# The low part of every second ffn_down k-tile: an accumulating DMA onto the negated high part instead of a VectorE subtraction

## The chip, the cores and the metric

The kernel runs on one core of one Trainium2 chip. The metric is the device time of one execution, in microseconds (us). The kernel before takes 2200.96 us, the median of three runs (2200.92 to 2201.33). The engines are named as the profile names them: PE is TensorE (PEld its weight loads), ACT is ScalarE, DVE is VectorE, POOL is GpSimd, and SP is SyncE, whose queue issues the loads. "q" behind a name (SPq) is the engine's queue.

## The reference

Two layers of a bidirectional encoder over 256 tokens with 2048 channels, all in float32. Each layer adds two normed branches to the residual: a mixer of four parallel head groups between one input and one output projection, and a dense SwiGLU feed-forward of hidden width 5632. The change concerns the last product of the feed-forward alone:

```python
h = rmsnorm(x, norm_ffn_pre[l])
f = (jax.nn.silu(h @ ffn_gate[l]) * (h @ ffn_up[l])) @ ffn_down[l]
x = x + rmsnorm(f, norm_ffn_post[l])
```

`ffn_down[l]` is 5632 x 2048 in float32, 46 MB for each layer.

## The kernel before

All large products are made in float32r, a shortened float32, which the program's own estimate counts at a quarter of float32's time. To keep the precision, each operand is split into a high part (the value rounded to float32r) and a low part (what is left), and three products are summed: high by high, high by low, low by high. The weights stream through once from DRAM, and are split on the way:

- A *raw* tile holds two k-tiles of 128 rows by 1024 columns, 1 MB in all. SP issues its load (line 214). There are three raw tiles (`NRAW`).
- A *unit* is one k-tile with 1024 columns. `half` says which half of its raw tile it is: 0 or 1. Its high part, named `whi`, is a copy by ACT with conversion (line 227). Its low part, named `wlo`, is for ffn_down a subtraction by DVE, raw minus high (line 236). There are seven buffers of each (`NSPLIT`).
- A *step* is one unit's products with one of the two token tiles: six matmuls of 128x128 by 128x512 into two PSUM banks. In each bank the first matmul takes `whi`, the second takes `wlo`, and at the end the low part of the activations (`hT`) meets `whi` again.

In ffn_down the units run in groups of four. A group's four units are multiplied with token tile 0, then with token tile 1, so eight steps make a group. A unit's buffers come free after its step with token tile 1. Numbering the units of a group 4g to 4g+3, the buffers of unit 4g go to unit 4g+7, and so on. There are 176 units of ffn_down in the program: 2 layers, 2 halves of the output columns (`pair`), 44 k-tiles. So there are 44 groups, 22 in a row in each layer, and 88 units with `half` 1.

The order of the work on each engine is written out by the program itself. `run` walks the steps; before each, `splits_to` splits as many units ahead as there are free buffers. It emits the high part of unit n, then the low part of unit n-1. After the low part of a unit with `half` 1, `lo_next` emits the load that goes into the raw tile just finished, three raw tiles on:

```python
self.split_lo(self.units[self.next_lo])
self.next_lo += 1
if self.next_lo % 2 == 0:
    self.loads_to(self.next_lo // 2 + NRAW)
```

Each engine works through its own list in order, and waits are on data and buffers alone. So ACT's next high part waits until PE has finished with a buffer; DVE's low part waits for the high part; SP's load waits until the raw tile's last reader is done; and in the first matmuls of a step PE waits for the unit's high and low parts. The engine wrappers (`Paced`) also keep an estimate of each engine's progress, by which small side work (transposes, norms) is put between the products. Line 89 of the profile is the call in that wrapper, so nearly all compute instructions carry it, and rows are told apart by their tiles.

Of the kernel before, what the change touches and what calls it, by code (L numbers as in the profile page):

```python
# [11 lines left out]
F32 = mybir.dt.float32  # L12
F32R = mybir.dt.float32r
AF = mybir.ActivationFunctionType
ALU = mybir.AluOpType
# [19 lines left out]

SLOTS = 14  # 8 KB tiles for activations and what one mixer needs
NRAW = 3  # loads of two k-tiles of weights
NSPLIT = 7  # units of weights, split
RAMP = 3  # units split ahead at the start
CONV_LEAD = 1.5  # DVE's queue is filled up to here with the convolution's taps  # L40
LATENCY = 0.4  # from the end of side work to what depends on it
LC_AT = 12
STATS_AT = 20
IN_ORDER, OUT_ORDER = "BCADV", "CBAD"  # groups of w_in's columns, of w_out's rows
# Units by group: a group's products with one token tile follow those with the other.
START, FIRST, REGULAR, LAST = [2, 2, 4, 4, 4], [6, 5, 5], [4, 4, 4, 4], [4, 4, 3, 5]
# The first transposes of x: before which step, of which token tile and chunk
FIRST_X = ((0, 0, 0), (1, 1, 0), (6, 0, 1), (10, 1, 1), (13, 0, 2), (17, 1, 2), (21, 0, 3), (25, 1, 3))


class Unit:
    """One k-tile of weights for 1024 output columns."""

# [5 lines left out]
class Raw:  # L59
    """Two k-tiles of weights as they come from DRAM: parts are (columns' AP, width)."""  # L60

# [5 lines left out]
class Step:  # L67
    """One unit's products with one token tile, for some of its two banks."""

# [6 lines left out]
class Paced:  # L76
    """An engine that keeps an estimate of when its instructions so far will be done."""

# [24 lines left out]
class Trunk:  # L103
# [25 lines left out]

# [1 line left out]
    def name(self, s):  # L131
# [24 lines left out]

# [1 line left out]
    def spend(self, engine, op, n, args, kw):  # L158
# [26 lines left out]

# [1 line left out]
    def rsqrt(self, out, sums, n, inv):  # L187
        """out = (sums * inv + EPS) ** -0.5"""
        nc = self.nc
        m = self.small(n, "ms")  # L190
        nc.vector.tensor_scalar(m, sums, inv, EPS, op0=ALU.mult, op1=ALU.add)
        nc.gpsimd.tensor_tensor(out, m, self.mhalf[:, 0:n], op=ALU.pow)

    def split_hi_lo(self, dst, src):
        """dst[:, 0], dst[:, 1] = the float32r part of src, and what is left."""
        hi, lo = dst
        self.nc.scalar.activation(hi, src, AF.Copy)
        self.nc.vector.tensor_tensor(lo, src, hi.bitcast(F32), op=ALU.subtract)

# [1 line left out]
    def load(self, r, between):  # L201
        """Two k-tiles in one transfer for each part, or in two with other loads between them."""
        r.tile = self.wp.tile([P, 2, 1024], F32, tag="raw", bufs=NRAW, name=self.name("raw"))
        off = 0
        for ap, width in r.parts:
            src = ap[r.k * P:(r.k + 2) * P, :].rearrange("(k p) n -> p k n", p=P)
            dst = r.tile[:, :, off:off + width]
            if between:
                self.nc.sync.dma_start(dst[:, 0:1], src[:, 0:1])
                for f in between:  # L210
                    f()
                self.nc.sync.dma_start(dst[:, 1:2], src[:, 1:2])
            else:
                self.nc.sync.dma_start(dst, src)
            off += width
# [15 lines left out]
    def split_lo(self, u):  # L231
        self.chain = 0.0
        u.lo = self.wp.tile([P, 1024], F32R, tag="lo", name=self.name("wlo"))
        w, gain, hi = u.raw.tile[:, u.half, :], u.raw.gain, u.hi.bitcast(F32)
        if gain is None:
            self.nc.vector.tensor_tensor(u.lo, w, hi, op=ALU.subtract)
        else:
            self.nc.vector.scalar_tensor_tensor(
                u.lo, w, gain[:, u.k:u.k + 1], hi, op0=ALU.mult, op1=ALU.subtract
            )  # L240

    def splits_to(self, n, needed):
        """Splits weights up to unit n; the low part of one goes with the high part of the next."""
        n = min(n, len(self.units))
        while self.next_split < n:
            r = self.next_split // 2
            self.loads_to(r + 1)
            self.split_hi(self.units[self.next_split])
            if self.next_split > self.next_lo:
                self.lo_next()  # L250
            self.next_split += 1
        while self.next_lo < min(needed + 1, n):
            self.lo_next()
# [29 lines left out]
    def lhs(self, phase, k, tok):  # L283
        """The stationary operand, its two parts, and what must have been made before."""
        kind, l = phase
# [27 lines left out]

# [1 line left out]
    def spawn(self, g):  # L315
        self.gens.append([g, 0.0])

    def tick(self):
        """Carries each piece of side work on whose last instructions should be done by now."""
        todo, self.gens = self.gens, []  # L320
# [18 lines left out]
    def fill(self):  # L339
        """The convolution's taps, where DVE would have to wait otherwise."""  # L340
        if self.conv_work and self.at["DVE"] < self.at["PE"] + CONV_LEAD:
# [20 lines left out]

# [1 line left out]
    def constants(self):  # L364
# [12 lines left out]
    def tables(self):  # L377
        """Rotary tables and the window, from the host."""
        t = self.cp.tile([P, 832], F32, name="tables")
# [35 lines left out]

# [1 line left out]
    def square_sum(self, src, out, n=(512,), bias=0.0):  # L417
# [3 lines left out]
    def transpose_x(self, phase, tok, c):  # L421
        """Chunk c (4 k-tiles) of token tile tok of x, into xT."""
        nc = self.nc
# [39 lines left out]
    def first_x(self):  # L463
        """The first transposes, each some steps before its products, then the statistics."""
        def stats(tok):
# [8 lines left out]

# [1 line left out]
    def squares(self, phase, pair, tok, b):  # L476
# [10 lines left out]
    def post_banks(self, phase, pair, tok, banks):  # L487
        """Squares and gained values of a pair's banks."""
        for b in banks:
# [39 lines left out]

# [1 line left out]
    def ffn_half(self, phase, j, tok):  # L531
# [18 lines left out]

# [1 line left out]
    def layer_consts(self, l):  # L552
        """What one layer's mixer needs beside the weights, in one slot."""
        nc, a = self.nc, self.a
# [40 lines left out]
    def load_bias(self, l):  # L595
        """Relative position bias by query, head and key, keys of a row from the last to the first."""
        nc = self.nc
# [16 lines left out]

    # group B: convolution
    def glu(self, phase, pair, tok):
# [73 lines left out]
    def conv_norm(self, t, y, dst):  # L690
        """dst = silu(layer norm of y over the channels), one token tile, channels first."""
        nc, v = self.nc, self.v
# [27 lines left out]

    # rotated q and k of group A
    def rope_a(self, phase, pair, tok):
# [25 lines left out]
    def heads_transposed(self, dst, src, n):  # L748
        """dst[:, h, tok] = src(tok)[:, h] transposed, for n heads."""
        nc = self.nc  # L750
# [10 lines left out]
    def exps(self, p, src, nm, sm, scale):  # L761
        """p = exp(scale * src + nm), with its sums."""
        for t in range(T):
# [3 lines left out]
    def probs_transposed(self, p, dst):  # L767
        """dst[key, key tile, query] of p[query, query tile, key]."""
        nc = self.nc
# [51 lines left out]

    # group C
    def norm_c(self, phase, pair, tok):
# [46 lines left out]
    def softmax(self, p, src, scale):  # L870
        """p = softmax(scale * src) by row; two stages."""
        nc = self.nc
# [9 lines left out]
    def values(self, dst, h, v, pt):  # L882
        """dst[:, hi|lo, h] = the output of one head, transposed."""
        nc = self.nc
# [30 lines left out]

    # group D
    def evac_d(self, phase, pair, tok):
# [42 lines left out]

    # values of groups A and D, the last columns of w_in
    def evac_v(self, phase, pair, tok):
# [54 lines left out]

# [1 line left out]
    def with_rstd(self, phase, tok, g):  # L1019
# [14 lines left out]

# [1 line left out]
    def build(self):  # L1036
# [60 lines left out]
def shape_tables():  # L1097
    """Rotary tables and the columns' window: they depend on shapes alone."""
    f = np.float32
# [22 lines left out]
def by_partition(x, n):  # L1122
    """(..., n * 128) as (..., 128, n)"""
    return x.reshape(*x.shape[:-1], n, P).swapaxes(-1, -2)
# [28 lines left out]
```

## Time and profile before

| | us |
|---|---|
| median of three runs | 2200.96 |
| span of the profiled execution | 2199.3 |
| PE busy in it | 2177.8 |
| DVE busy | 1259.3 |
| ACT busy | 1095.4 |
| POOL busy | 28.6 |

The span runs from the first instruction of the profiled execution to its last; no other time of that execution is given. The median of the runs is 1.66 us above the span. Matmuls are pipelined, so one of them lasts longer than the distance to the next, and PE's busy time is where matmuls are under way. A wait is idle time of an engine, put down to what released it last. "To landing" is the time from a DMA's issue to its completion. The granted clock of PE, PEclk, is shown as a share of its full speed.

### The profile page before, as it was taken

Reading aid. Unit: us, or ns where it says so; the run is one execution under the profiler, and the core shown is the slowest. Engines: PE = TensorE matmul, PEld = TensorE weight load, DVE = VectorE, ACT = ScalarE, POOL = GpSimd, SP = SyncE. Lnnn points to the kernel's source line nnn. Section 1 sums busy time; section 2 is a strip of 40 time slices with the busy share of each in tenths; the row PEclk is TensorE's granted clock in tenths of the full one; section 3 lists DMA queues with packets and bytes.
Section 4 is the critical chain, followed back from the end, with each engine's and each line's share of the span. In section 5 each row is a group of like instructions: output and inputs, shape, how many; then the busy total and the mean of one; then the engine's idle time right before and its main releaser. Section 6 shows DMA issues by size and latency. Waiting matters only on the chain.

```text
span 2199.3 us, 25310 instructions
## 1 busy us (share of the span) xinstructions
PE 2177.8 (99%) x9896; PEld 1797.7 (82%) x9896; DVE 1259.3 (57%) x1498; ACT 1095.4 (50%) x1420; POOL 28.6 (1%) x38
## 2 busy tenths in 40 slices
PE   8999999999999999999999999999999999999998
PEld 6888887888888888888878888878888888888886
DVE  5898455545555554444478975565555555544444
ACT  5556655544444444343465576455444444443432
POOL 0000000000000000000000000000000000000000
PEclk9999999999999999999999999999999999999999
DMA  7556445655555555555565553655555555555553
GB/s 280 197 173 187 159 165 200 223 193 188 183 189 191 191 191 191 211 191 191 211 236 191 182 181 134 227 186 202 191 190 191 192 191 192 191 192 211 191 209 135
DMA packets 170007, 424.43 MB, mean 193 GB/s; under 512 B 18592, under 2 KB 19104, under 8 KB 167584
## 3 DMA queue, kind: packets, MB, share of 16 engines
q1 hardware_dynamic: 169744, 422.79, 55.7%
q8 instruction: 77, 1.26, 0.2%
q14 instruction: 42, 0.34, 0.0%
q10 hardware_dynamic: 144, 0.03, 0.0%
HBM read 414.40 MB, written 8.39 MB: 192 GB/s over the span
## 4 chain that ended last, share of the span: by engine, by line
PE 96%; ACT 1%; DVE 1%; DMA 1%; issue 0%; SPq 0%; DVEq 0%; POOLq 0%; ACTq 0%
PE acc L89 91%; PE tp L89 4%; PE sc L89 1%; DMA raw<-in_w_in_dram 1%; ACT whi L89 1%; DVE xT L89 0%; ACT workA L89 0%; DVE x L89 0%; ACT xT L89 0%; ACT L89 0%; DVE mx L89 0%; DVE wlo L89 0%; ACT conv L89 0%; ACT qkD L89 0%; ACT junk L89 0%
## 5 line engine op out<-in xcount | busy, mean ns | idle before, releaser
L89 PE MATMUL acc<-whi,xT 128*128 128x512 f32 x4096 | 1304.7, 394 | 7.7 <-ACT xT L89 3.1
L89 PEld LDWEIGHTS acc<-whi,xT 128*128 128x128 f32 x4096 | 769.3, 188 | 172.6 <-DVE xT L89 5.5
L89 DVE SCALAR_TENSOR_TENSOR wlo<-raw,gains,whi 128x1024 fp32r<-128x1024 f32 x512 | 651.7, 1281 | 344.3 <-ACT whi L89 331.0
L89 ACT ACTIVATE whi<-raw,gains 128x1024 fp32r<-128x1024 f32 x512 | 586.3, 1152 | 472.4 <-PE acc L89 448.8
L89 PE MATMUL acc<-wlo,xT 128*128 128x512 f32 x2048 | 799.4, 390 | 0.5 <-DVE wlo L89 0.5
L89 DVE TENSOR_TENSOR wlo<-raw,whi 128x1024 fp32r<-128x1024 f32 x240 | 293.5, 1224 | 274.0 <-ACT whi L89 256.2
L89 PEld LDWEIGHTS acc<-wlo,xT 128*128 128x128 f32 x2048 | 385.3, 188 | 77.2 <-DVE wlo L89 1.0
L89 PE MATMUL acc<-whi,hT 128*128 128x512 f32 x1408 | 434.5, 389 | 0.0
L89 ACT ACTIVATE whi<-raw 128x1024 fp32r<-128x1024 f32 x240 | 254.2, 1061 | 313.8 <-PE acc L89 313.7
L89 PEld LDWEIGHTS acc<-whi,hT 128*128 128x128 f32 x1408 | 264.3, 188 | 54.9
L89 PE MATMUL acc<-wlo,hT 128*128 128x512 f32 x704 | 273.9, 389 | 0.0
L89 PEld LDWEIGHTS acc<-wlo,hT 128*128 128x128 f32 x704 | 132.1, 188 | 27.4
L89 DVE SCALAR_TENSOR_TENSOR conv<-uT,lc,conv 128x256 f32<-128x256 f32 x240 | 99.2, 477 | 0.0
L89 DVE SCALAR_TENSOR_TENSOR h<-acc,rstd,h 128x512 f32<-128x512 f32 x44 | 33.0, 751 | 115.1 <-ACT h L89 114.5
L89 ACT ACTIVATE h<-acc,rstd 128x512 f32<-128x512 f32 x44 | 30.3, 689 | 81.7 <-PE acc L89 81.4
L89 DVE TENSOR_TENSOR hT<-tp,hT 128x512 fp32r<-128x512 f32 x44 | 30.4, 691 | 41.1 <-ACT hT L89 41.1
L89 ACT ACTIVATE junk<-acc 128x512 bf16<-128x512 f32 x32 | 19.0, 595 | 55.4 <-PE acc L89 53.3
L89 PE MATMUL acc<-whi,mixC 128*128 128x512 f32 x128 | 44.7, 402 | 0.0
L89 ACT ACTIVATE hT<-tp 128x512 fp32r<-128x512 f32 x44 | 25.8, 587 | 33.7 <-PE tp L89 33.7
L89 PE MATMUL acc<-whi,mixB 128*128 128x512 f32 x128 | 42.2, 397 | 0.0
L89 DVE TENSOR_TENSOR mg<-acc,gpost 128x512 f32<-128x512 f32 x32 | 21.4, 686 | 36.0 <-PE acc L89 19.3
L89 PE MATMUL acc<-whi,mixD 128*128 128x512 f32 x128 | 41.6, 391 | 0.0
(137 smaller groups left out, 978.1 us busy)
## 6 DMA issues: line engine op xcount, KB each, us to landing
raw<-in_ffn_gate_dram SPq DMA_DIRECT2D x176, 512.0 KB, 3.8
raw<-in_ffn_up_dram SPq DMA_DIRECT2D x176, 512.0 KB, 4.9
raw<-in_ffn_down_dram SPq DMA_DIRECT2D x88, 1024.0 KB, 5.0
raw<-in_w_in_dram SPq DMA_DIRECT2D x63, 1024.0 KB, 5.1
raw<-in_w_out_dram SPq DMA_DIRECT2D x32, 1024.0 KB, 5.0
raw<-in_w_in_dram SPq DMA_DIRECT2D x34, 512.0 KB, 4.6
x_spill<-x SPq DMA_DIRECT2D x6, 1024.0 KB, 8.2
x<-x_spill SPq DMA_DIRECT2D x6, 1024.0 KB, 9.1
```

Source lines behind the costliest of these rows:

```text
L89: return f(*args, **kw)
```

## The change

Outside this hunk the diff only removes comments. In ffn_down, units with `half` 1 no longer have their low part made by DVE. ACT writes the negated high part into the `wlo` buffer (a second copy with conversion of the raw tile, with scale -1), and then POOL issues a DMA that reads the raw tile in SBUF and adds it onto that buffer in SBUF: raw minus high.

```diff
         w, gain, hi = u.raw.tile[:, u.half, :], u.raw.gain, u.hi.bitcast(F32)
-        if gain is None:
+        if gain is None and u.phase[0] == "down" and u.half == 1:
+            self.nc.scalar.activation(u.lo, w, AF.Copy, scale=-1.0)
+            self.tc.nc.gpsimd.dma_start(u.lo.bitcast(F32), w, accum_op=ALU.add)
+        elif gain is None:
             self.nc.vector.tensor_tensor(u.lo, w, hi, op=ALU.subtract)
```

On ACT in the middle of layer 0's ffn_down, these rows stand before. `whi` is a high part, `raw` the raw tile it comes from, and two rows in a row share a raw tile (half 0, half 1):

```order
L89 ACTIVATE whi_6870<-raw_6792 128x1024
L89 ACTIVATE whi_6880<-raw_6816 128x1024
L89 ACTIVATE whi_6916<-raw_6816 128x1024
L89 ACTIVATE whi_6926<-raw_6862 128x1024
L89 ACTIVATE whi_6938<-raw_6862 128x1024
L89 ACTIVATE whi_6948<-raw_6884 128x1024
```

At the same place these stand now (the tiles have other numbers):

```order
L89 ACTIVATE whi_6884<-raw_6804 128x1024
L89 ACTIVATE whi_6894<-raw_6829 128x1024
L89 ACTIVATE wlo_6896<-raw_6804 128x1024
L89 ACTIVATE whi_6931<-raw_6829 128x1024
L89 ACTIVATE whi_6941<-raw_6876 128x1024
L89 ACTIVATE wlo_6943<-raw_6829 128x1024
L89 ACTIVATE whi_6954<-raw_6876 128x1024
L89 ACTIVATE whi_6964<-raw_6899 128x1024
L89 ACTIVATE wlo_6966<-raw_6876 128x1024
```

The negated copy of a raw tile's second unit (`wlo_6896` from `raw_6804`) stands behind the high part of the next unit, which comes from the next raw tile (`whi_6894` from `raw_6829`).

On SP, the loads of ffn_down with what they wait for, before (DVE's semaphore, and DMAHW, the completions of earlier SP transfers):

```order
L214 DMA raw_6884<-in_ffn_down_dram 128x2x1024 [waits DMAHW0_49,DVE_49]
L214 DMA raw_6930<-in_ffn_down_dram 128x2x1024 [waits DMAHW2_49,DVE_49]
L214 DMA raw_6952<-in_ffn_down_dram 128x2x1024 [waits DMAHW3_49,DVE_49]
L214 DMA raw_6998<-in_ffn_down_dram 128x2x1024 [waits DMAHW4_49,DVE_49]
L214 DMA raw_7020<-in_ffn_down_dram 128x2x1024 [waits DMAHW5_49,DVE_49]
```

The same loads now (DMASW is the completion of a DMA that POOL issued):

```order
L214 DMA raw_6899<-in_ffn_down_dram 128x2x1024 [waits DMASW6_49,DMAHW0_49,DVE_49,Activation_49]
L214 DMA raw_6946<-in_ffn_down_dram 128x2x1024 [waits DMASW7_49,DMAHW2_49,DVE_49,Activation_49]
L214 DMA raw_6969<-in_ffn_down_dram 128x2x1024 [waits DMASW0_49,DMAHW3_49,DVE_49,Activation_49]
L214 DMA raw_7016<-in_ffn_down_dram 128x2x1024 [waits DMASW1_49,DMAHW4_49,DVE_49,Activation_49]
L214 DMA raw_7039<-in_ffn_down_dram 128x2x1024 [waits DMASW2_49,DMAHW5_49,DVE_49,Activation_49]
```

Each load of a raw tile now waits for the accumulating DMA that reads that tile. The order of the loads on SP is the same. In all, 88 subtractions leave DVE's list, 88 copies come into ACT's and 88 DMAs into POOL's; on PE a transpose of the side work moves by one step at one place in each layer.

## Rows read from the trace of the kernel before

**Rows 1.** The page: busy time by engine, and the chain by engine and line.

```profile
PE 2177.8 (99%) x9896; PEld 1797.7 (82%) x9896; DVE 1259.3 (57%) x1498; ACT 1095.4 (50%) x1420; POOL 28.6 (1%) x38
...
PE 96%; ACT 1%; DVE 1%; DMA 1%; issue 0%; SPq 0%; DVEq 0%; POOLq 0%; ACTq 0%
PE acc L89 91%; PE tp L89 4%; PE sc L89 1%; DMA raw<-in_w_in_dram 1%; ACT whi L89 1%; DVE xT L89 0%; ACT workA L89 0%; DVE x L89 0%; ACT xT L89 0%; ACT L89 0%; DVE mx L89 0%; DVE wlo L89 0%; ACT conv L89 0%; ACT qkD L89 0%; ACT junk L89 0%
```

**Rows 2.** Busy time by engine in stretches: layer 0's ffn_down, layer 1's, half groups.

```profile
core 0: us, PE busy (x) PEld busy (x) DVE busy (x) ACT busy (x) POOL busy (x), PEclk, DMA share, GB/s
859.80:1099.00 239.20, 239.20 (x1061) 198.07 (x1060) 111.82 (x99) 97.04 (x102) 0.55 (x1) 1.00 0.55 202
1950.40:2190.00 239.60, 239.60 (x1060) 198.40 (x1059) 111.14 (x99) 93.28 (x99) 0.55 (x1) 1.00 0.53 193
...
955.84:961.28 5.44, 5.44 (x26) 4.50 (x25) 4.46 (x4) 3.01 (x3) 0.00 (x0) 1.00 0.60 206
961.28:966.72 5.44, 5.44 (x26) 4.50 (x25) 0.45 (x1) 1.24 (x2) 0.00 (x0) 1.00 0.44 179
```

**Rows 3.** ACT in order of time, one group of ffn_down: start us, us, what, [idle before].

```profile
954.30 1.06 ACT L89 ACTIVATE whi<-raw 128x1024 fp32r<-128x1024 f32 x1 [5.74 <-PE acc L89]
955.66 1.06 ACT L89 ACTIVATE whi<-raw 128x1024 fp32r<-128x1024 f32 x1 [0.30 <-PE acc L89]
957.02 1.06 ACT L89 ACTIVATE whi<-raw 128x1024 fp32r<-128x1024 f32 x1 [0.30 <-PE acc L89]
958.38 1.06 ACT L89 ACTIVATE whi<-raw 128x1024 fp32r<-128x1024 f32 x1 [0.30 <-PE acc L89]
965.18 1.06 ACT L89 ACTIVATE whi<-raw 128x1024 fp32r<-128x1024 f32 x1 [5.74 <-PE acc L89]
```

**Rows 4.** The costliest groups of the page, the split without a gain.

```profile
L89 DVE TENSOR_TENSOR wlo<-raw,whi 128x1024 fp32r<-128x1024 f32 x240 | 293.5, 1224 | 274.0 <-ACT whi L89 256.2
...
L89 ACT ACTIVATE whi<-raw 128x1024 fp32r<-128x1024 f32 x240 | 254.2, 1061 | 313.8 <-PE acc L89 313.7
```

**Rows 5.** DVE in order of time, the same group.

```profile
955.39 5.31 DVE L89 TENSOR_TENSOR wlo<-raw,whi 128x1024 fp32r<-128x1024 f32 x4 [5.57 <-ACT whi L89]
```

**Rows 6.** SP's queue in order of time, the same group, first load.

```profile
956.65 0.37 SPq L214 DMA_DIRECT2D raw<-in_ffn_down_dram  x1
```

**Rows 7.** PE in order of time, eight microseconds on.

```profile
961.81 0.84 PE L89 MATMUL acc<-whi,hT 128*128 128x512 f32 x3
962.49 0.39 PE L89 MATMUL acc<-wlo,hT 128*128 128x512 f32 x1
```

**Rows 8.** What SP's queue waited for, 860 to 1080 us: total, times, longest.

```profile
SPq L214 <- DVE wlo L89: 201.2, 41, 7.8
```

**Rows 9.** DMA issues: count, KB each, median us to landing.

```profile
raw<-in_ffn_gate_dram SPq DMA_DIRECT2D x176, 512.0 KB, 3.8
...
raw<-in_ffn_down_dram SPq DMA_DIRECT2D x88, 1024.0 KB, 5.0
...
x<-x_spill SPq DMA_DIRECT2D x6, 1024.0 KB, 9.1
...
out_dram<-x SPq DMA_DIRECT2D x8, 256.0 KB, 2.3
```

**Rows 10.** DMA issues between 1045 and 1062 us, where other transfers run beside the loads.

```profile
raw<-in_ffn_down_dram SPq DMA_DIRECT2D x3, 1024.0 KB, 7.0
```

**Rows 11.** POOL's instructions by tile: duration ns min/median/max.

```profile
L89 POOL TENSOR_TENSOR pr<-ms,mhalf x8: 549/553/559, 359.0 to 2192.2; 128x1 f32<-128x1 f32 x8
...
L89 POOL TENSOR_TENSOR f<-ms,mhalf x4: 1497/1898/2299, 104.3 to 1200.9; 128x6 f32<-128x6 f32 x4
```

## The prediction

> **What bounds the kernel now.** I read the page's busy times and the chain of waits first [rows 1]: PE is busy 99% of the span and carries 96% of the chain that ended last, nearly all of it in the accumulating products. DVE's low parts have a rounded 0% of the chain. Then I read the two stretches of ffn_down by engine [rows 2]. PE is busy 239.20 of 239.20 us and 239.60 of 239.60, at the full granted clock (1.00, the upper of its two levels, 2.4 GHz). There PE never waits, and no other engine can make it quicker. DVE is busy less than half of these stretches, and before the subtractions it idles on ACT's high parts [rows 4]. Last I read one group in order of time, since the change adds a transfer in a ring of waits, and what matters is how much room that ring has.
>
> ACT makes four high parts in a burst, one each 1.36 us as PE frees buffers, and the burst comes again after 965.18 - 954.30 = 10.88 us [rows 3]. That is the period of a group: 8 steps of 1.36 us. The first of the four, after the long idle time, is unit 4g+7, since it takes the buffers of unit 4g; it has half 1. DVE takes four subtractions of 1.22 us [rows 4], starting at 955.39 [rows 5], so this unit's low part is done at 956.62, and SP's load of the raw tile that it frees starts at 956.65 [rows 6]. That SP waits for DVE each time is in its waits (201.2 us in 41 waits) [rows 8]; these cost nothing now, because the load lands 5.0 us after its issue [rows 9], at 961.65, and the first unit from it is split at 955.66 + 10.88 = 966.54. The room is 4.9 us.
>
> **The change part by part.**
>
> *DVE.* 88 subtractions of 1.224 us go, 107.7 us of busy time [rows 4]. They hide behind PE, which is busy throughout [rows 2], so the gain is 0. The most that could be gained is what the chain holds of DVE's low parts, less than half a per cent of 2199 us.
>
> *ACT.* 88 copies come in. They are the same copy as the high part, so 1.06 us each [rows 3], 93 us in all. ACT idles 5.74 us in each group [rows 3] and gets 2.12 us more to do, so its busy time alone costs nothing. Its order counts: the negated copy of unit n (half 1) stands behind the high part of unit n+1, which comes from the next raw tile. For unit 4g+7 the copy runs from 955.66 + 1.06 = 956.72 to 957.78.
>
> *POOL's DMA.* It may start at 957.78. Call A the time from the end of ACT's copy to the landing of the sum. Two users wait for it.
>
> First PE. Unit 4g+7 is multiplied first six steps after its buffers came free. The last of the three matmuls at 961.81 opens that step (0.23 us from one to the next), and its first matmul with `wlo` is at 962.49 [rows 7]. So PE stalls if A exceeds 962.49 - 957.78 = 4.7 us. All products behind it wait, since PE's list is in order.
>
> Second SP, and this is the stricter one. The raw tile of units 4g+6 and 4g+7 is now free only when the DMA has landed. Its next load holds units 4g+12 and 4g+13. ACT's high part of 4g+12 waits for that load, and the negated copy of 4g+11 is queued behind it on ACT, then POOL's DMA for 4g+11. That is a closed ring from one group to the next: A, the load (5.0), a high part (1.06), a copy (1.06), and about 0.1 for starts and semaphores. The ring takes T = A + 7.2 us, with a load that lands as now. It fits into 10.88 us only if A is at most 3.7. Beyond it every group starts later than the one before, until PE runs at the ring's pace. The other unit with half 1 in each group, 4g+9, has a ring of the same length. The loads behind a waiting load on SP (norm gains and residual reloads among them) wait too, and have more room.
>
> *What A is.* The trace before has no accumulating DMA and none issued by POOL, so I bound it. From below: the shortest data transfer that is listed, 256 KB of output, lands in 2.3 us [rows 9]; with A = 2.3 the ring is 9.5 us and nothing changes. A 512 KB load, the bytes of our source, lands in 3.8 us [rows 9]; T would be 11.0, 0.12 too much. From above: 1 MB reloads of the residual land in 9.1 us beside other loads [rows 9]; T would be 16.3. The addition has to read two operands of 512 KB, and the row with that many bytes read is the 1 MB load at 5.0 us [rows 9]. POOL issues it, which no row prices; POOL's own instructions take 0.55 to 1.9 us [rows 11], and I add 1.0. I take A = 6.0, so T = 13.2 and the excess is 2.32 us a group.
>
> The Trainium skill has a price for such a transfer. "DMA: Bandwidth & Descriptors", section "Anatomy of one DMA — SWDGE (gpsimd) path", gives a DMA from POOL a fixed 2.0 us and the bytes at 436 GB/s: 3.2 us for 512 KB, an estimate by that page, which would leave the ring at 10.4 us and the kernel unchanged. The 3.8 and 5.0 us of 512 KB and 1 MB in [rows 9] show the page's slope (1.2 us for 512 KB), but a fixed part of 2.6 us on SP's queue. Against that estimate stands "Collectives: The Full Stack", Part 3, "Why ReduceScatter is half of AllGather": a reducing transfer goes at half the rate because it reads two sources, not because the addition is slow. By both pages A is 4.4 us, an estimate, T is 11.6 and the kernel about 2232 us. No row of this trace shows a reducing transfer.
>
> *Contention.* The 16 DMA engines are busy 0.55 of these stretches [rows 2], 6.0 us of each group. Two transfers that read 1 MB each bring that towards 11 of 13.2 us, so transfers will meet. Where others run beside the loads now, they land after 7.0 us instead of 5.0 [rows 10]. I take a fifth of that, 0.4 us a group.
>
> *The sum.* A layer has 22 groups in a row, so 21 links of the ring; two layers have 42. 42 x 2.32 = 97 us. The first stall of each layer is 6.0 - 4.7 = 1.3 us, 3 us for both. Contention is 42 x 0.4 = 17 us. Together 117 us, 2199.3 + 117 = 2316 for the span, and with the 1.66 us by which the median stands above the span, 2318 us. The bounds of A give, without contention, 2201 us (A up to 3.7), 2206 (3.8), and 2201 + 42 x 5.42 + 2 x 4.4 = 2437 (9.1).
>
> **The rivals.**
>
> *The DMA is hidden: not slower, 2201 us.* If A is at most 3.7 us the ring closes within the group's 10.88 us and PE never sees it. For it: the 256 KB row at 2.3 us, a transfer within SBUF that never touches DRAM, and idle DMA engines in part of each group (share 0.44 in its second half [rows 2]). Against it: even a plain 512 KB load takes 3.8 us, and this transfer reads twice as much. It decides at A = 3.7. This is also how the page's 3.2 us would come out.
>
> *The accumulating DMAs become the bound: up to about 2545 us.* If the transfer itself keeps all 16 DMA engines as long as the slowest row suggests, 9.1 - 2.6 = 6.5 us, then a group asks 6.0 + 2 x 6.5 = 19 us of them, 8.1 us over the period, and 42 x 8.1 = 341 us come on top. For it: an addition in the data path is nowhere priced here. Against it: the 9.1 us row is one of transfers that share the engines with loads. A fall of PE's granted clock in repeated stalls would also count here, since PE's steps stand between the landing and ACT's next high part; it stood at its upper level through both stretches [rows 2], and I give it no price of its own.
>
> *The relief of DVE pays: about 2195 us.* The side work at the ends of ffn_down (norm, residual, transposes) would come sooner on a freer DVE. For it: DVE is in the chain there. Against it: low parts have a rounded 0% of the chain [rows 1], and the added waits stand in the same stretches.
>
> That the change doesn't do what it says is excluded by the instruction lists: 88 subtractions less on DVE, 88 copies more on ACT, 88 DMAs on POOL.
>
> **How the numbers follow.** About 0.2%, 4.4 us, is what a measurement of this kernel can tell from no change. The forecast (the ring sets the pace, A between 3.8 and 9.1) gets 0.73, the hidden transfer 0.09, the DMA engines as the bound 0.16, a gain 0.02. Slower by over 0.2% holds the forecast and the DMA-bound case: 0.89. Within 0.2% is the hidden one: 0.09. Faster is 0.02. The range of 8 in 10 leaves out the lower end of A with the hidden case and the upper half of the DMA-bound case: 2225 (A of about 4.25 with no contention) to 2470 (A = 9.1 with contention and some more).
>
> **What would show it right or wrong.** Right: in both stretches of ffn_down PE waits about once a group, for the accumulating DMA, 2 to 3 us each; ACT's high parts wait for loads instead of PE; SP's loads wait for POOL's DMAs; the group's period is 13 to 14 us where it was 10.88, and everything outside ffn_down is unchanged. The time from the end of ACT's negated copy to the landing is A, 6 us if the main term is right. Wrong: PE still busy without gaps in ffn_down (A below 3.7), or a DMA share near 1.0 there with a longer period (the engines are the bound).

## The result, and the profile after

The changed kernel takes 2409.94 us, the median of four runs (2405.46 to 2423.14), against 2200.95 for the kernel before: a ratio of 1.0959, 95% interval 1.0931 to 1.0988. The loss is 209 us; 117 were forecast. (Ratios leave out an execution that lies over 1.5% above the fastest of its kernel; there is one here, named where it stands.) In the profiled execution (span 2409.4) the loss lies in ffn_down alone. Over the first 859.5 us, before layer 0's ffn_down, PE is busy 849.94 us, and 849.88 before. Between the two ffn_downs, from the same instruction on POOL on, the stretches agree too, before and now (as [rows 2]):

```profile
1124.73:1941.90 817.17, 815.40 (x3733) 673.47 (x3732) 492.44 (x614) 427.54 (x568) 12.76 (x13) 1.00 0.56 190
```

```profile
1239.82:2057.00 817.18, 815.42 (x3733) 673.46 (x3733) 491.18 (x613) 428.77 (x569) 12.79 (x13) 1.00 0.56 190
```

The page after, as [rows 1], and the issues and queue of the new DMA with the loads beside it, as [rows 9] (the queue's last column is the share of 16 engines' span):

```profile
PE 2240.8 (93%) x9896; PEld 1826.8 (76%) x9896; DVE 1151.9 (48%) x1410; ACT 1171.0 (49%) x1508; POOL 105.1 (4%) x126
...
PE 69%; DMA 22%; ACT 4%; DVE 3%; issue 2%; SPq 0%; ACTq 0%; POOL 0%; DVEq 0%; POOLq 0%
...
raw<-in_ffn_down_dram SPq DMA_DIRECT2D x88, 1024.0 KB, 6.4
...
wlo<-raw POOLq DMA_DIRECT2D x88, 512.0 KB, 5.5
...
q0 software_dynamic: 12672, 46.14, 10.4%
```

PE's share of the chain has gone from 96 to 69%, and DMAs now hold 22%. DVE's busy time fell by 107.4 us, and the kernel has nothing of it. The waits say what PE waits for in the whole run, and what SP and ACT wait for in layer 0's stretch (860 to 1200 us), each with total, times and longest:

```profile
PE acc L89 <- DMA wlo<-raw: 147.0, 53, 7.2
```

```profile
SPq L214 <- DMA wlo<-raw: 321.4, 43, 12.7
```

```profile
ACT whi L89 <- DMA raw<-in_ffn_down_dram: 114.3, 28, 7.7
```

PE waits 147 us for the accumulating DMA, 2.8 us in the mean, and is busy 63 us longer (2240.8 against 2177.8) with the same 9896 matmuls; together that is the 210 us. Most of the 63 is the clock: the mean granted clock of the run is 0.973 and was 0.999, by which 2177.8 us become about 2236 (an estimate). SP's loads wait for that DMA, ACT's high parts for the loads: the ring that was foreseen. In [rows 8] SP waited for DVE, with room to spare.

The groups run at two paces. Here are the two in the chain of waits, first a group of layer 1 where each DMA of the ring starts as the loads before it end (start us, us, what):

```profile
2108.11 4.53 DMA wlo<-raw
...
2112.78 6.17 DMA raw<-in_ffn_down_dram
...
2119.06 1.07 ACT whi L89
...
2120.15 1.22 DVE wlo L89
2121.37 4.52 DMA wlo<-raw
```

That is one turn of the ring: 2121.37 - 2108.11 = 13.3 us. And here is layer 0 at the slow pace:

```profile
955.65 9.26 DMA wlo<-raw
...
964.95 6.96 PE acc L89 x17
...
971.99 1.07 ACT whi L89
...
973.08 1.21 DVE wlo L89
974.29 8.95 DMA wlo<-raw
...
983.37 7.77 DMA raw<-in_ffn_down_dram
...
991.25 1.07 ACT whi L89
...
993.56 7.87 DMA wlo<-raw
```

Here a turn is 18.6 and then 19.3 us, since the same DMA lands after 7.9 to 9.3 us instead of 4.5. (The first of these turns runs over PE's matmuls, not over a load.) The issues around 955.7 us go with it: a load is issued 0.19 us after POOL's start (955.84), and both take longer.

```profile
raw<-in_ffn_down_dram SPq DMA_DIRECT2D x1, 1024.0 KB, 6.6
wlo<-raw POOLq DMA_DIRECT2D x1, 512.0 KB, 9.3
```

The two paces by engine, 39 us of the first and 73 us of the second:

```profile
887.59:927.05 39.46, 34.13 (x141) 27.11 (x140) 7.36 (x7) 17.86 (x19) 5.22 (x7) 0.96 0.86 240
955.65:1029.15 73.50, 53.08 (x190) 41.79 (x189) 11.00 (x11) 25.46 (x29) 6.96 (x9) 0.84 0.74 172
```

The DMA share is lower at the slow pace (0.74 against 0.86), yet the engines are not idle while the two transfers move. Here are that meeting and the 2 us behind it (as the rows above), and the queues that moved data in it, SP's (hardware) from 958 to 960 us and POOL's (software) from 962 to 963.6:

```profile
958.00:964.00 6.00, 1.44 (x7) 0.86 (x5) 0.35 (x1) 1.44 (x2) 0.00 (x0) 1.00 0.95 234
964.20:966.20 2.00, 1.25 (x3) 1.06 (x4) 0.67 (x1) 0.36 (x1) 0.87 (x1) 0.50 0.05 14
```

```profile
q1 hardware_dynamic: 139, 0.57, 92.6%
```

```profile
q0 software_dynamic: 81, 0.32, 99.0%
```

The load's packets go first and the accumulating DMA's almost wholly behind them. The next pair then starts together as well, and for about 2 us next to nothing moves. The starts of POOL's DMAs in layer 0 count the loss. Five groups take 13.4 us (862.85 to 929.88), one 16.7, seven and a half 18.3 (946.61 to 1083.78), four 13.8 and three 18.0. Against 10.88 us that is 5 x 2.5 + 5.9 + 7.5 x 7.4 + 4 x 2.9 + 3 x 7.1 = 107 us in layer 0, half of the 209. The slow pace begins where the norm gain's load stands in SP's queue (932.15) and again with the residual's reload (1140.23), and so it does in layer 1 (2140.65 and 2337.94). What ends it is not shown: the first pair's results leave PSUM from 1022.56 to 1031 us, and the groups stay slow until 1083.78.

### The profile page after: what moved, and what is told of

Read it like the earlier page. It is cut to its first block, busy times and chain, and to the rows that moved or that the text cites. A ratio compares the mean times of both kernels' runs of the same rounds, so it can differ in the third digit from the quotient of the medians.

```text
span 2409.4 us, 25721 instructions
## 1 busy us (share of the span) xinstructions
PE 2240.8 (93%) x9896; PEld 1826.8 (76%) x9896; DVE 1151.9 (48%) x1410; ACT 1171.0 (49%) x1508; POOL 105.1 (4%) x126
## 4 chain that ended last, share of the span: by engine, by line
PE 69%; DMA 22%; ACT 4%; DVE 3%; issue 2%; SPq 0%; ACTq 0%; POOL 0%; DVEq 0%; POOLq 0%
PE acc L89 65%; DMA wlo<-raw 11%; DMA raw<-in_ffn_down_dram 10%; PE tp L89 3%; ACT whi L89 2%; DVE wlo L89 2%; PE sc L89 1%; DMA raw<-in_w_in_dram 1%; ACT workA L89 0%; ACT L89 0%; ACT wlo L89 0%; DVE xT L89 0%; DVE mx L89 0%; DVE x L89 0%; ACT xT L89 0%
## 5 line engine op out<-in xcount | busy, mean ns | idle before, releaser
L89 PE MATMUL acc<-whi,hT 128*128 128x512 f32 x1408 | 467.3, 414 | 0.0
L89 DVE TENSOR_TENSOR wlo<-raw,whi 128x1024 fp32r<-128x1024 f32 x152 | 185.7, 1223 | 544.4 <-ACT whi L89 541.8
L89 PE MATMUL acc<-wlo,hT 128*128 128x512 f32 x704 | 301.2, 428 | 147.3 <-DMA wlo<-raw 147.0
L89 PEld LDWEIGHTS acc<-whi,hT 128*128 128x128 f32 x1408 | 287.0, 204 | 62.2
L89 PEld LDWEIGHTS acc<-wlo,hT 128*128 128x128 f32 x704 | 143.8, 204 | 201.1 <-DMA wlo<-raw 171.3
L237 POOL DMA_DIRECT2D wlo<-raw x88 | 76.4, 868 | 1514.3 <-ACT wlo L89 1377.3
L89 ACT ACTIVATE wlo<-raw 128x1024 fp32r<-128x1024 f32 x88 | 91.8, 1043 | 0.0
```

Source lines behind the costliest of these rows:

```text
L89: return f(*args, **kw)
L237: self.tc.nc.gpsimd.dma_start(u.lo.bitcast(F32), w, accum_op=ALU.add)
```

## The experiments

Theory: a ring of waits (DMA lands, raw tile free, load lands, next high part, copy, DMA) sets the pace, its length decided by whether the accumulating DMA shares its time with a load. Rivals: the DMA engines are simply full; PE's own wait for the landing is all; ACT's added copy costs time. Each run is timed beside the kernel before on the same chip.

**The copy right behind its own high part.** In `splits_to`:

```diff
                 self.lo_next()
+            u = self.units[self.next_split]
+            if u.phase[0] == "down" and u.half == 1:
+                self.lo_next()
             self.next_split += 1
```

> The negated copy of a half-1 unit is emitted right behind the unit's own high part, not behind the next unit's, so it no longer waits for the next raw tile's load. Ring theory (copy, DMA, raw tile, load, next copy is a ring of waits, and its length is the period): the ring now spans six units instead of four (16.3 us of room instead of 10.88), and the landing, about 5 us after a copy that ends at 956.4 in the old time, comes before PE's need at 962.5: 2201 to 2215 us, PE without gaps in ffn_down but for a few. Rival 1 (the 16 DMA engines are the bound): the traffic is the same, so 2300 us or more, DMA share still 0.78. Rival 2 (PE waits for the DMA's own latency, whatever the order): 2300 us or more, with stalls once a group.

Measured: 2256.74 us, ratio 1.0255 (1.0237 to 1.0272). Three quarters of the loss is gone by order alone, with the same transfers, so neither their traffic nor their latency as such made that part. But the time lies above the expected 2201 to 2215 us, and the window shows what is short now:

```profile
870.00:1080.00 210.00, 195.57 (x843) 158.22 (x842) 46.60 (x40) 107.85 (x114) 31.06 (x36) 0.99 0.97 275
```

With the ring opened the 16 DMA engines are busy at a share of 0.97. They are close to being the bound, as the first rival said, only at a much faster pace than the changed kernel's. But that is not all of the time left: most groups take 11 to 13 us by POOL's starts, one takes 16 where the gain's load comes (926.9 to 943.0) and one 17 where the residual is reloaded (1069.1 to 1086.1).

**The DMA reads the high part.** The raw tile is then free without it.

```diff
-            self.tc.nc.gpsimd.dma_start(u.lo.bitcast(F32), w, accum_op=ALU.add)
+            self.tc.nc.gpsimd.dma_start(u.lo.bitcast(F32), hi, accum_op=ALU.add)
```

> The accumulating DMA reads the unit's high part instead of the raw tile (same bytes, same order, PE still waits for it; the low part of these units is then zero and not raw minus high). The raw tile is free after ACT's copy. Ring theory: without the raw tile the load drops out of the ring, what is left is landing, two steps of PE, the next high parts, copy, about A + 6.0 us against 10.88, with A near 5 to 6: 2201 to 2250 us. Rival (PE's wait for the landing alone, or the DMA engines, made the time): 2350 us or more.

Measured: 2489.99 us, ratio 1.1313 (1.1296 to 1.133), a miss in the other direction. The loads did come free earlier, but at the very moment at which the DMA starts, so that the transfers met loads throughout (the median DMA lands after 9.5 us). The issues around 967.8 us, then the chain:

```profile
raw<-in_ffn_down_dram SPq DMA_DIRECT2D x1, 1024.0 KB, 6.4
wlo<-whi POOLq DMA_DIRECT2D x1, 512.0 KB, 9.1
```

```profile
967.90 9.09 DMA wlo<-whi
...
977.03 3.92 PE acc L89 x9
...
980.99 4.16 issue
...
985.16 9.38 DMA wlo<-whi
```

This ring has no load in it: landing, PE's next steps, high parts and copy ("issue", 4.2 us), 17.3 us in all. What was wrong in the expectation was to take the landing as 5 to 6 us whatever runs beside it. In the changed kernel the wait for the raw tile also kept some loads out of the DMA's way.

**The extra loads moved.**

```diff
-            self.steps[n0 + 40].pre += [lambda l=l: self.load_post("norm_ffn_post", l)]
-            self.steps[n0 + 140].pre += [lambda: self.reload_x(self.xd)]
+            self.steps[n0 + 80].pre += [lambda l=l: self.load_post("norm_ffn_post", l)]
+            self.steps[n0 + 172].pre += [lambda: self.reload_x(self.xd)]
```

> The changed kernel with the load of the post norm's gain moved from step 40 to step 80 of ffn_down and the residual's reload from step 140 to 172. Theory: the groups of 18.4 us (accumulating DMA and load always in flight together, landing after 9.2 us) begin when such an extra transfer shifts the two rings against each other, and end at the next pair's start; without it the groups stay at 13.2 us, so about 44 x 2.4 = 105 us over the kernel before and a little more: 2300 to 2330 us. Rival (the rings drift there by themselves, or the engines saturate): 2390 to 2415 us, as the changed kernel.

Measured: 2337.09 us, the median of three runs (2335.18 to 2341.13), ratio 1.0622 (1.0604 to 1.064); a fourth took 2377.07 and is left out. That is 7 us above the expected range and 73 below the changed kernel. In the profiled run the groups stay at the quick pace through the stretch (from 887.88 to 1083.48, fourteen groups in 195.6 us, 14.0 each, one of them 18.5 where the gain is loaded and the pair ends), and the medians to landing are near those of the quick pace:

```profile
raw<-in_ffn_down_dram SPq DMA_DIRECT2D x88, 1024.0 KB, 6.1
...
wlo<-raw POOLq DMA_DIRECT2D x88, 512.0 KB, 4.9
```

So the slow pace was set off by those loads, and in this run nothing drifts there by itself. Of the excess over 2330, PE's two waits of 6.3 us in all behind the gain, which now comes late, are a part.

**The traffic without a reader.** DVE subtracts as before, and the DMAs go from the high part into a scratch tile.

```diff
-            self.nc.scalar.activation(u.lo, w, AF.Copy, scale=-1.0)
-            self.tc.nc.gpsimd.dma_start(u.lo.bitcast(F32), w, accum_op=ALU.add)
+            self.nc.vector.tensor_tensor(u.lo, w, hi, op=ALU.subtract)
+            self.tc.nc.gpsimd.dma_start(self.scratch, hi, accum_op=ALU.add)
...
```

Left out here are the scratch tile itself and one of two buffers of a small temporary, given up for it.

> The low parts are DVE's as in the kernel before; POOL issues the same 88 accumulating DMAs of 512 KB, from the high part into a scratch tile that nobody reads (one buffer less for a small temporary). Ring theory: traffic without anybody waiting costs nothing, 2200 to 2208 us. Rival (contention of the DMA engines with the weight loads is the cost): loads land later than 10 us and the time is 2250 us or more.

Measured: 2253.29 us, ratio 1.0237 (1.0222 to 1.0252): the rival's time, but the loads land after 5.3 us in the median and not after 10. The run does not tell the two apart as meant: the DMAs keep the high part's buffer, so ACT waited for them after all (waits of ACT in layer 0's stretch), and the engines were full (window):

```profile
ACT whi L89 <- DMA scratch<-whi: 121.1, 29, 10.4
```

```profile
900.00:1100.00 200.00, 190.50 (x810) 152.94 (x810) 79.16 (x69) 67.44 (x73) 27.88 (x32) 0.98 0.97 272
```

What it does show is that 88 such transfers beside the loads fill the DMA engines, at a time close to that of the run with the copy first (2257).

**A plain copy instead of the addition.**

```diff
-            self.tc.nc.gpsimd.dma_start(u.lo.bitcast(F32), w, accum_op=ALU.add)
+            self.tc.nc.gpsimd.dma_start(u.lo.bitcast(F32), w)
```

> POOL's DMA copies the raw tile onto the low part instead of adding (the low part of these units is then the raw value); order, waits and bytes of the source are the changed kernel's. If the second operand's read is what the DMA engines pay for, a transfer alone should land in about 3.3 us instead of 4.55 and keep the 16 engines some 1.5 us instead of 2.85; the ring is then about 3.6 + 5.5 + 2.3 = 11.4 us where it runs undisturbed and some 14 us beside loads: 2225 to 2290 us. Rival (a DMA issued by POOL costs this whatever it does): landing 4.5 us and more, 2390 us or more.

Measured: 2355.77 us, ratio 1.0702 (1.0683 to 1.072), between the two expectations. The queue's share and the two kinds of landing (all 88, and one alone near 954 us):

```profile
q0 software_dynamic: 12672, 46.14, 4.8%
...
wlo<-raw POOLq DMA_DIRECT2D x88, 512.0 KB, 6.2
```

```profile
wlo<-raw POOLq DMA_DIRECT2D x1, 512.0 KB, 2.9
```

The engine time of one transfer is 0.048 x 2353.7 / 88 = 1.28 us; with the addition it was 0.104 x 2409.4 / 88 = 2.85 us. The addition a little more than doubles it. Alone the copy lands in 2.9 us. But in this order most of them met a load (the median lands after 6.2 us), and most groups took 14 to 15 us. Even a transfer that is half as dear loses 155 us inside this ring.

**Every fourth unit, the order of the change.**

```diff
-        if gain is None and u.phase[0] == "down" and u.half == 1:
+        if gain is None and u.phase[0] == "down" and u.k % 4 == 1:
```

> Only unit 4g+1 of each group takes the negated copy and the accumulating DMA (44 instead of 88), in the changed kernel's order; the others are DVE's. PE needs this unit's low part only 11 us after it can be made, and the DMA engines have room (about 6.1 + 2.7 = 8.8 of 10.88 us). Ring theory: the ring through raw tile, load, next copy is there and takes 4.9 + 5.2 + 2.2 = 12.3 us against 10.88; after a few groups that eat PE's slack, PE runs at its pace: 2235 to 2265 us. Rival (only PE's own wait for the landing counts, or only the DMA engines' load): 2201 to 2206 us.

Measured: 2284.90 us, ratio 1.0384 (1.0368 to 1.0399), 20 us above the expected range. This is the clearest sight of the ring. There is one DMA a group, it lands in 4.5 us, the engines' share is 0.68 to 0.70, PE had 11 us of room at the start, and still the period is 12.7 us:

```profile
991.81 4.55 DMA wlo<-raw
...
996.50 5.78 DMA raw<-in_ffn_down_dram
...
1002.36 1.07 ACT whi L89
...
1004.66 4.51 DMA wlo<-raw
```

4.55 + 5.78 + 1.07 + 1.2 and the starts between make 12.85. No wait of PE alone and no full DMA engine explains it.

**Every fourth unit, the copy right behind its own high part.** The two edits together.

> As the run with every fourth unit, but its negated copy is emitted right behind its own high part, not behind the next one's. Ring theory: the load is no longer in front of the copy, nothing closes within a group, and the DMA engines have room: 2200 to 2206 us. Rival (the DMA's latency or traffic as such costs time): as the other order, 2235 us or more.

Measured: 2238.71 us, ratio 1.0170 (1.0155 to 1.0186). The number is the rival's; the stretch up to the gain's load did as the theory expected. POOL's starts:

```profile
905.39 0.87 POOL L237 DMA_DIRECT2D wlo<-raw  x1 [10.01 <-ACT wlo L89]
916.27 0.87 POOL L237 DMA_DIRECT2D wlo<-raw  x1 [10.01 <-ACT wlo L89]
...
948.91 0.87 POOL L237 DMA_DIRECT2D wlo<-raw  x1 [10.01 <-ACT wlo L89]
963.48 0.87 POOL L237 DMA_DIRECT2D wlo<-raw  x1 [13.71 <-ACT wlo L89]
```

Up to 948.91 the period is the kernel before's own 10.88 us: PE is busy 54.40 of 54.40 us from 894.50 on, at a DMA share of 0.78, so traffic and latency as such cost nothing there. The DMA at 916.27 lands in 4.6 us. SP issues the gain's load at 921.46; the DMAs at 927.15, 938.03 and 948.91 then land after 7.8, 9.0 and 11.5 us, and the ten groups from 948.91 to 1071.0 take 12.2 us in the mean.

**The same, the extra loads moved.** As in the run with moved loads.

> Every fourth unit, copy right behind its own high part, with the gain's load moved to step 80 and the residual's reload to 172. Theory: the groups run at 10.88 us, with nothing lost, until the extra load shifts the weight loads onto the accumulating DMAs; that now comes at step 80 instead of 40, so five groups more in each layer are free, and the gain comes late for the first pair's end (about 10 us in all, as in the run of all units with moved loads): 2220 to 2240 us, and groups of 10.88 us up to step 80. Rival (the collision comes by itself after some groups): longer groups and landings over 7 us from the seventh group on, as with the load at step 40.

Measured: 2236.74 us, ratio 1.0164 (1.0147 to 1.0181), inside the expected range. The groups run at 10.88 us up to step 80 (starts at 959.54 and 970.42, then 988.88, where POOL's DMA was held up behind the late gain), with landings under 6.1 us. So the collision came with the disturbance and not with the count of groups. After it the landings grow again, by about 1 us a group, to 9.4 us four groups on. The total is only 2 us below the run before, as PE now waits 8.7 us for the late gain.

**All units, the copy first, and the extra loads moved.** The edits of the first and the third run.

> All 88 units, the copy right behind its own high part, and the gain's load and the residual's reload moved to steps 80 and 172. What is left should be the DMA engines: at a share of 0.98 they need about 11.5 us for a group's two loads and two accumulating DMAs, 44 x 0.6 = 27 us over the kernel before: 2225 to 2240 us. Rival (the remaining time is PE's wait for a landing that takes longer than its 6 us of room): no better than 2250 us.

Measured: 2256.53 us, ratio 1.0259 (1.0243 to 1.0274), the same as without moving. The expectation failed, and the rival's number came out. PE's waits for the DMA fell from 37.0 to 26.6 us, but it waited 11.8 us behind the gain that came late. POOL's starts divide the loss of layer 0: nine groups before that stall (873.5 to 977.5) and nine behind it (998.6 to 1102.7) take 11.6 us each, at DMA shares of 0.96 and 0.97, and the one with the stall takes 21.1. Against 10.88 that is 12 us and 10 us of the 28 that a layer loses. That the engines' rate makes the 12 fits these shares, but no run shows it by itself.

**ACT's copy alone, DVE adds.**

```diff
-            self.tc.nc.gpsimd.dma_start(u.lo.bitcast(F32), w, accum_op=ALU.add)
+            self.nc.vector.tensor_tensor(u.lo, w, u.lo.bitcast(F32), op=ALU.add)
```

> The changed kernel's negated copy on ACT, in the changed order, but DVE adds the raw tile onto it instead of a DMA. Theory (ACT's extra copy and its place alone cost nothing; the ring needs the DMA's landing to be too long): the ring is 1.2 + 5.0 + 2.5 = 8.7 us against 10.88, 2200 to 2204 us. Rival (ACT's 93 us more, or its order, are part of the loss): 2215 us or more.

Measured: 2200.90 us, ratio 1.0001 (0.9991 to 1.0010). ACT's 88 copies and their place in its order cost nothing:

```profile
859.80:1099.00 239.20, 239.20 (x1061) 198.06 (x1060) 109.83 (x101) 132.95 (x146) 0.55 (x1) 1.00 0.57 202
```

PE is busy all the time while ACT has 36 us more than in [rows 2]. No version beat the kernel before: where PE never waits, none could.

## Why the prediction was right, and where its size was off

- *DVE's relief is worth 0*: right. 107.4 us left DVE, and no stage became quicker.
- *ACT's busy time and place cost nothing by themselves*: right, shown by the run in which DVE adds.
- *The ring through raw tile and load, stricter than PE's own wait*: right. With every fourth unit it holds PE at 12.7 us where nothing else is short, and moving the copy one place up opens it (in the undisturbed groups of the run with every fourth unit, 10.88 us). At the slow pace the ring through PE is about as long: a turn shown above runs over it.
- *A, the landing*: right in the middle and wrong as one number. It was taken as 6.0 us for every group, with a ring of 13.2. The median landing is 5.5 us from POOL's start, 5.8 from the copy's end, but that is the middle of two kinds. At the quick pace it is 4.5 to 5.5 us from POOL's start. The load then takes 5.8 to 7.6 instead of 5.0, since the other unit's DMA still moves as it is issued (from 2112.7 to 2115.5 us POOL's queue holds the engines at 97% and SP's at 10%), and the ring is 13.3: the forecast pace, by two errors that cancel. Where a load starts with it, the landing takes 7.9 to 9.9 us and the ring 18.3.
- *Contention, 0.4 us a group*: mis-sized, and about the whole shortfall of 92 us. The forecast saw that transfers would meet, but priced a meeting by a fifth of the delay in [rows 10], as if meetings were scattered. They are not: in this ring each DMA's landing releases the next load just as the other unit's DMA starts, so once shifted they meet every time. It measured about 5 us a group in 18.5 of the 40.5 groups counted in both layers (10.5 in layer 0, 8 in layer 1), and the runs with moved loads show that this part was set off by two extra loads in each layer, which the forecast named only as having "more room".
- *The range*: it held the time partly by luck. Its upper part was worked out from A = 9.1 in every group with a load that lands as before (2437). A group at the slow pace costs more than that, since the load takes longer too: 44 groups of 18.3 us would make about 2527 (an estimate, 2201 + 44 x 7.4), above the range. Only about half of them were slow.
- *The hidden transfer*: excluded; even the plain copy, 2.9 us alone, did not stay hidden. *The DMA engines as the bound*: not over a group of the changed kernel (0.74 to 0.86), though they are full while two transfers meet (0.95); by their share the next limit once the order is mended (0.97).
- *The Trainium skill*: the A of 4.4 us, an estimate from "DMA: Bandwidth & Descriptors" (section "Anatomy of one DMA — SWDGE (gpsimd) path") and "Collectives: The Full Stack" (Part 3, "Why ReduceScatter is half of AllGather") of the Trainium skill, is near the 4.5 us measured for a transfer alone. The trace agrees with the second page's half rate for a reducing transfer, 2.85 against 1.28 us of engine time; that the second read makes it, and not the addition, no run here shows. The 2232 us worked out from the 4.4 failed in the ring's load, which lands later even at the quick pace, and in the meetings.
- *PE's clock*, which was given no price: it falls in the long stalls (last section) and makes most of PE's 63 us more. They are not all loss, since a quicker PE would wait longer where the ring runs over a load. In the run that reads the high part PE is on the ring (granted clock 0.57 from 977 to 981 us); in the changed kernel a load ends at about the same moment, and no run separates it.

## What to carry to other kernels

Work that leaves an engine which the critical path never waits for is worth nothing, and a transfer that replaces it brings a landing time into every ring of buffers it holds: add up that ring (landing, next load, what is queued in front of the next issue) against the period before anything else. In-order queues decide how long the ring is: here one copy placed in front of instead of behind the next tile's conversion took back three quarters of the loss. And do not price a meeting of transfers as an accident: in this periodic kernel they locked into meeting every time, and a single extra load was enough to set that off.

## What the runs showed that was not expected

PE's granted clock in the stalls. Over 7 us behind a wait of 5.5 us it is this (as [rows 2]):

```profile
964.00:971.00 7.00, 6.05 (x14) 4.84 (x15) 0.87 (x1) 1.51 (x2) 0.87 (x1) 0.51 0.70 170
```

0.51 of full speed is the lower of the two levels, 1.2 GHz; 17 matmuls take 6.96 us there. At the quick pace, with stalls of 2 to 3 us, the mean stays at 0.96.

A DMA that meets a load does not share evenly: the load lands after 6.4 to 6.6 us instead of 5.0, the accumulating DMA after 9.1 to 9.3 instead of 4.5. The accumulating DMA pays most of the meeting. At the quick pace the order is the other way round: there the load comes second, and lands after 5.8 to 7.6 us.

The chain puts DVE's subtraction in front of POOL's DMA, since it ends at the moment at which POOL starts. That is chance. With the copy first, ACT's copy at 979.28 ends at 980.32 and DVE had been done since 979.68:

```profile
979.28 1.04 ACT L89 ACTIVATE wlo<-raw 128x1024 fp32r<-128x1024 f32 x1
```

```profile
980.62 0.87 POOL L237 DMA_DIRECT2D wlo<-raw  x1 [3.23 <-ACT wlo L89]
```

POOL starts 0.30 us after the copy's end in both orders (in the changed kernel at 2121.37, after a copy that ends at 2121.07), with DVE at work or not.
